# Modulation weights of the second layer in 256 KB pieces, four steps ahead, in a two-layer SSD and S5 block

## The chip, the cores and the metric

The kernel runs on one core of a Trainium2 chip. The metric is the device time of one launch in microseconds (us), as the median of the runs shown. TensorE (PE) does the matrix products, with its weight loads listed apart as PEld; VectorE (DVE), ScalarE (ACT) and GpSimd (POOL) work on tiles in SBUF; SyncE (SP) issues nearly all DMA transfers, in order, and stands still in front of a transfer until its destination is free.

## The reference

Two layers work on 1024 latent tokens and 256 context tokens of width 1024, all in float32. Each layer first turns the conditioning vectors into six modulation vectors, then runs a mixer (SSD and S5 scans) and a gated feed-forward network. What the change touches is the first line, for layer 1:

```python
def ada_params(cvec, w, b):
    return jnp.split(jax.nn.silu(cvec) @ w + b, 6, axis=-1)

sh1, sc1, gt1, sh2, sc2, gt2 = ada_params(c, w_ada[l], b_ada[l])
csh1, csc1, cgt1, csh2, csc2, cgt2 = ada_params(c_ctx[None, :], w_ada[l], b_ada[l])
...
hx = modulate(rmsnorm(x, g_pre_ffn[l]), sh2, sc2)
x = x + gt2[:, None, :] * rmsnorm(conv_ffn(hx, ffn_w_up[l], ffn_conv_w[l], ffn_conv_b[l], ffn_w_down[l], rows), g_post_ffn[l])
```

`w_ada[l]` is 1024 by 6144, which is 24 MB in float32, and it is used for two rows alone (the latent and the context conditioning).

## The kernel before, in words

Large products are split: each operand becomes a high and a low part, and three matmuls (lines 751, 752, 753, called `mm` here) replace one. The feed-forward network of a layer runs over two blocks of tokens. In each block, groups of two or three column tiles of the up-projection (weights `rw`, split into `ws`) alternate with a down-projection of eight output tiles (weights `raw`, split into `wd` or a unit). In layer 0 the blocks have 640 tokens. Block 0's matmuls are 256 and 384 columns wide, block 1's 320.

The modulation of layer 1 is computed in the background of layer 0's feed-forward network: `ada` (line 668) is a generator, and `tick` (line 126), which the network calls once for every second weight tile of the up-projection and once for every output tile of the down-projection, moves it on by one `yield`. Line 1940 queues its first third (column blocks 0 to 3) in block 0, line 1982 the other two thirds (4 to 11) in block 1. Below, these are **stage one** and **stage two**.

A step of `ada` asks for a piece of `w_ada`, and multiplies a piece that was asked for `ahead` steps before. A piece has `n1` blocks of 128 rows by 512 columns. Each block is one matmul with a 128 by 32 stationary tile `cv` that occupies 32 of TensorE's 128 columns (`tile_position=(0, 32 * j)`, with j the block's number modulo 4). In the trace such a float32 matmul stands as two MATMUL records. Before, `n1` is 2 and `ahead` 1: 16 pieces of 512 KB in stage one and 32 in stage two, all into one tile `adaw` that has one buffer. Stage two has `gap` 1, so its steps are two ticks apart.

`self.unit(512)` takes the next of 33 numbered tiles of the activations' pool in SBUF from a list, and `free` puts it back at the list's end. The prologue already loads layer 0's first modulation blocks in that way (`n1` 1, `ahead` 16). Layer 0's other modulation blocks keep the form with `adaw`. A scheduler of the framework then fixes each engine's order of instructions at build time.

Of the kernel before, what the change touches and what calls it, by code (L numbers as in the profile page):

```python
# [98 lines left out]
class Kern:  # L99
# [1425 lines left out]
        return acc  # L1525


    def mods(self, l, cbs, which, par=False, gap=0):
        if par:
            yield from self.params(l, self.sp)  # L1530
        yield from self.ada(l, self.prs[l], cbs, 2, 1, gap)
        for w in which:
            self.modvec(self.prs[l], w)

# [127 lines left out]
    def layer(self, l, H):  # L1662
# [225 lines left out]
        n0, n1 = blks[0][1], blks[1][1]  # L1888
# [48 lines left out]
            fill(i, 100)  # L1937
        self.before = es
        if not last:
            self.bg.append(self.flag("A1", self.mods(1, range(4), ("A1",), True)))  # L1940
        self.fgn = 1 if last else 2
        self.fg = [self.stream(blks[1], md[0], R, pr["G1"], pr["A2"], pr["ada"][:, 24:32], hd[0], pn)]
        H = [[], []]
# [13 lines left out]
        def first_next():  # L1957

            ws.close()
            self.keep, self.tabs = self.open_keep(1), ExitStack()  # L1960
            pt = self.tabs.enter_context(self.pool("tp1", side="right"))
            pa = fs.enter_context(self.pool("s5a1"))

            def small():
                self.tp = yield from self.s5_tables(1, pt, pa)
            self.bg.insert(0, self.flag("s5", small()))
            for k in range(KT):
                H[0].append(self.split_act(load(1)(k), n1, g if k % 2 else nc.vector))
                if k == 5:
                    res.extend(self.residual(blks[1], lambda: self.unit(n1)))  # L1970
                yield
# [6 lines left out]
        if last:  # L1978
            self.fg.append(self.stream_out(blks[0], md[1], R[0], pr["G2"], pn))
            tail, done, fin = self.last_out(blks[1], R[0], pr["G2"], pn)  # L1980
        else:
            self.bg.append(self.mods(1, range(4, 12), ("G1", "A2", "G2"), False, 1))
            self.fg.append(self.stream(blks[0], md[1], R, pr["G2"], self.prs[1]["A1"], self.prs[1]["ada"], hd[1], pn))
            tail, done = first_next(), squares
        acc = self.ffn(l, blks[1], H2[1], LW, new, pr, pg, pw, 8, before, tail, done)
# [133 lines left out]
```

## Time and profile before

| | |
|---|---|
| median of 3 runs | 3443.62 us |
| all runs | 3463.33, 3443.62, 3442.58 us |
| the profiled execution | 3467.04 us |
| its span | 3465.3 us, 48617 instructions |
| mean granted TensorE clock | 0.934 |
| PE busy | 3088.8 us (89%) |
| DVE / ACT / POOL busy | 2060.4 / 1454.7 / 1104.2 us |
| `adaw` transfers | 80 of 512 KB, 48 of them for layer 1 |

The profiled execution is one run with its own time; the 1.7 us between its time and its span lie around the span. A row of the timeline gives the start of an instruction or of a run of equal ones, its length, and in brackets how long the engine had stood idle before it and what ended that. Starts of matmuls are measured; their ends are modelled.

### The profile page before, as it was taken

To read this page: it belongs to the slowest core of one execution; us is meant where nothing else is said; L and a number is where in the kernel's file an instruction comes from. 1 tells how busy PE (TensorE), PEld (TensorE's weight loads), DVE (VectorE), ACT (ScalarE), POOL (GpSimd) and SP (SyncE) were. 2 spreads that over 40 slices of the span, in tenths; PEclk is the share of its full clock that TensorE was granted. 3 is DMA by queue.
4 is the path that set the end of the run, shared out by engine and by line. 5 is a ranking of instruction groups with operands and counts; after the bars stand their busy time and mean duration, and the time that the engine had idled before them with its cause. 6 is when DMAs were issued, how large, how long until landed. Compare 5 with 4: busy or idle time off the path is not lost. (4 is left out here: it accounts for less than half of the span.)

```text
span 3465.3 us, 48617 instructions
## 1 busy us (share of the span) xinstructions
PE 3088.8 (89%) x18067; PEld 2673.7 (77%) x18067; DVE 2060.4 (59%) x3789; ACT 1454.7 (42%) x2610; POOL 1104.2 (32%) x847
## 2 busy tenths in 40 slices
PE   7689796898899999899999879775898999999998
PEld 4578674678879999889999769774576777877876
DVE  4875982456644444653344887993556655566555
ACT  4324522544543434543334443522545544454443
POOL 3651451213312323322222341451233333233230
PEclk8899897889999999999999889886889999999999
DMA  7345378525472222663322426268524533354332
GB/s 234 114 139 178 116 239 212 169 76 159 145 223 77 69 78 75 205 209 115 111 92 75 134 87 202 67 215 193 147 84 145 176 115 93 100 161 121 93 96 72
DMA packets 587281, 468.80 MB, mean 135 GB/s; under 512 B 59076, under 2 KB 506190, under 8 KB 587045
## 3 DMA queue, kind: packets, MB, share of 16 engines
q1 hardware_dynamic: 586565, 465.53, 44.5%
q8 instruction: 142, 2.33, 0.3%
q14 instruction: 94, 0.77, 0.1%
q0 software_dynamic: 480, 0.17, 0.0%
HBM read 355.99 MB, written 109.61 MB: 134 GB/s over the span
## 5 line engine op out<-in xcount | busy, mean ns | idle before, releaser
L860 POOL TENSOR_TENSOR ws<-rw,ws 128x512 fp32r<-128x512 f32 x352 | 483.9, 1377 | 1033.4 <-ACT ws L859 764.0
L752 PE MATMUL mm<-unit,ws 128*128 128x320 f32 (+3 forms) x2112 | 714.8, 338 | 3.4 <-POOL unit L901 3.4
L751 PE MATMUL mm<-unit,ws 128*128 128x320 f32 (+3 forms) x2112 | 716.5, 339 | 0.2 <-ACT unit L900 0.2
L753 PE MATMUL mm<-unit,ws 128*128 128x320 f32 (+3 forms) x2112 | 713.5, 338 | 0.0
L1439 DVE SCALAR_TENSOR_TENSOR fc<-fr,fcols,fc 128x255 f32<-128x255 f32 (+2 forms) x220 | 207.3, 958 | 492.7 <-ACT fc L1432 492.7
L751 PE MATMUL mm<-unit,whi 128*128 128x320 f32 (+3 forms) x1264 | 429.1, 341 | 38.0 <-ACT unit L900 23.4
L753 PE MATMUL mm<-unit,wlo 128*128 128x320 f32 (+3 forms) x1264 | 421.1, 334 | 31.4 <-POOL ub L996 19.0
L751 PEld LDWEIGHTS mm<-unit,ws 128*128 128x128 f32 x2112 | 398.0, 188 | 46.6 <-issue 10.1
L752 PEld LDWEIGHTS mm<-unit,ws 128*128 128x128 f32 x2112 | 398.0, 188 | 36.1 <-POOL unit L901 4.6
L753 PEld LDWEIGHTS mm<-unit,ws 128*128 128x128 f32 x2112 | 397.9, 188 | 34.7 <-issue 3.4
L752 PE MATMUL mm<-unit,whi 128*128 128x320 f32 (+3 forms) x1264 | 421.8, 334 | 2.6 <-POOL unit L901 1.6
L742 POOL TENSOR_TENSOR wlo<-raw,whi 128x1024 fp32r<-128x1024 f32 (+1 forms) x86 | 230.6, 2682 | 361.9 <-ACT whi L741 328.2
L751 PEld LDWEIGHTS mm<-unit,whi 128*128 128x128 f32 x1264 | 253.0, 201 | 74.7 <-ACT unit L900 25.4
L859 ACT CAST ws<-rw 128x512 fp32r<-128x512 f32 x352 | 218.4, 621 | 206.0 <-PE mm L753 116.8
L753 PEld LDWEIGHTS mm<-unit,wlo 128*128 128x128 f32 x1264 | 253.6, 201 | 47.3 <-POOL ub L996 19.2
L1519 DVE TENSOR_TENSOR acc<-mm,acc 128x256 f32<-128x256 f32 (+2 forms) x336 | 185.0, 554 | 171.2 <-PE mm L753 170.3
L752 PEld LDWEIGHTS mm<-unit,whi 128*128 128x128 f32 x1264 | 254.1, 201 | 15.3 <-issue 6.0
L751 PE MATMUL mm<-g,wd 128*128 128x320 f32 (+3 forms) x708 | 243.7, 345 | 10.8 <-ACT wd L859 6.8
L753 PE MATMUL mm<-g,wd 128*128 128x320 f32 (+3 forms) x708 | 241.5, 343 | 6.5 <-DVE wd L860 6.3
L752 PE MATMUL mm<-g,wd 128*128 128x320 f32 (+3 forms) x708 | 242.0, 342 | 0.0
L895 ACT COPY fr<-mm 128x320 f32<-128x320 f32 (+3 forms) x264 | 125.2, 476 | 195.1 <-PE mm L753 194.8
L1441 DVE SCALAR_TENSOR_TENSOR fc<-fr,fcols,fc 128x255 f32<-128x255 f32 (+2 forms) x220 | 176.0, 815 | 3.5
(390 smaller groups left out, 5761.5 us busy)
## 6 DMA issues: line engine op xcount, KB each, us to landing
rw<-in_ffn_w_up_dram SPq DMA_DIRECT2D x352, 256.0 KB
adaw<-in_w_ada_dram SPq DMA_DIRECT2D x80, 512.0 KB
raw<-in_ffn_w_down_dram SPq DMA_DIRECT2D x96, 384.0 KB
raw<-in_w_in_dram SPq DMA_DIRECT2D x40, 512.0 KB
raw<-in_w_out_dram SPq DMA_DIRECT2D x32, 512.0 KB
unit<-in_w_ada_dram SPq DMA_DIRECT2D x32, 256.0 KB
wt<-ws SPq DMA_DIRECT2D x32, 256.0 KB
ct<-w SPq DMA_DIRECT2D x64, 128.0 KB
```

Of the source, the lines that this page charges most:

```text
L742: (eng or nc.vector).tensor_tensor(lo[:, :m], raw[:, :m], hi[:, :m].bitcast(F32), op=OP.subtract)
L751: mm(ps, whi[:, k], ahi[:, sl], start=first and k == 0, stop=False)
L752: mm(ps, whi[:, k], alo[:, sl], start=False, stop=False)
L753: i = mm(ps, wlo[:, k], ahi[:, sl], start=False, stop=last and k == len(a) - 1)
L859: self.nc.scalar.copy(hi, x)
L860: eng.tensor_tensor(lo, x, hi.bitcast(F32), op=OP.subtract)
L895: self.nc.scalar.copy(t[:, o:o + c], x)
L1439: v.scalar_tensor_tensor(cr[:, :, 1:], rr[:, :, :w - 1], f[0][:, ft:ft + 1], cr[:, :, 1:], op0=OP.mult, op1=OP.add)
L1441: v.scalar_tensor_tensor(cr[:, :, :w - 1], rr[:, :, 1:], f[2][:, ft:ft + 1], cr[:, :, :w - 1], op0=OP.mult, op1=OP.add)
L1519: v.tensor_tensor(acc[m][:, o:o + c], ps, acc[m][:, o:o + c], op=OP.add)
```

## The change: four arguments of one generator

`mods` gets two parameters that it hands to `ada`, and the two calls for layer 1 set them to pieces of one block (256 KB) in units, four steps ahead, with one tick for each step in stage two as well. The call for layer 0 keeps the defaults.

```diff
-    def mods(self, l, cbs, which, par=False, gap=0):
+    def mods(self, l, cbs, which, par=False, gap=0, n1=2, ahead=1):
         if par:
             yield from self.params(l, self.sp)
-        yield from self.ada(l, self.prs[l], cbs, 2, 1, gap)
+        yield from self.ada(l, self.prs[l], cbs, n1, ahead, gap)
...
-            self.bg.append(self.flag("A1", self.mods(1, range(4), ("A1",), True)))
+            self.bg.append(self.flag("A1", self.mods(1, range(4), ("A1",), True, 0, 1, 4)))
...
-            self.bg.append(self.mods(1, range(4, 12), ("G1", "A2", "G2"), False, 1))
+            self.bg.append(self.mods(1, range(4, 12), ("G1", "A2", "G2"), False, 0, 1, 4))
```

The order of instructions differs from layer 0's feed-forward network's first group to the end of stage two, and nowhere else. On PE, stage two, in a down-projection of block 1, the kernel before has (`adaw` is the 512 KB tile, `g` and `wd` or `unit` the operands of the down-projection):

```order
L753 MATMUL mm<-g,wd 128x320
L55 MATMUL ps<-adaw,cv 32x512 x2
L751 MATMUL mm<-g,wd 128x320
L752 MATMUL mm<-g,wd 128x320
L753 MATMUL mm<-g,wd 128x320
```

The next such pair follows 36 `mm` rows later. The changed kernel has there, on PE:

```order
L753 MATMUL mm<-g,unit 128x320
L55 MATMUL ps<-unit,cv 32x512
L751 MATMUL mm<-g,wd 128x320
L752 MATMUL mm<-g,wd 128x320
L753 MATMUL mm<-g,wd 128x320
```

The next one follows 18 `mm` rows later: the two members of a pair are pulled apart. Counted over all of PE's order, the 96 modulation matmuls of layer 1 stand in 48 places before, two in each. Now stage one has 25 places (one with six, two with two, the rest with one) and stage two 59 (five with two, the rest with one).

On PE, stage one, two pieces of the difference. The first is in the first down-projection, which has four modulation pairs before and none now:

```order
 L752 MATMUL mm<-g,unit 128x384
 L753 MATMUL mm<-g,unit 128x384
-L55 MATMUL ps<-adaw,cv 32x512 x2
 L751 MATMUL mm<-g,wd 128x256
 L752 MATMUL mm<-g,wd 128x256
```

The second is in the up-projection behind it, which now begins the stage with the place of six:

```order
-L752 MATMUL mm<-unit,ws 128x256
-L753 MATMUL mm<-unit,ws 128x256
-L751 MATMUL mm<-unit,ws 128x256
+L55 MATMUL ps<-unit,cv 32x512 x6
 L752 MATMUL mm<-unit,ws 128x256
 L753 MATMUL mm<-unit,ws 128x256
```

The first modulation matmul moved from the end of the first up-projection to the second up-projection; the `mm` rows with a minus stand elsewhere in the change.

On SP, stage one, around the first down-projection (`raw`: its weights):

```order
-L55 DMA adaw<-in_w_ada_dram 128x2x512
-L1477 DMA raw<-in_ffn_w_down_dram 128x2x256
+L1477 DMA raw<-in_ffn_w_down_dram 128x2x256
+L55 DMA unit<-in_w_ada_dram 128x512 x2
 L1477 DMA raw<-in_ffn_w_down_dram 128x3x256
```

A request for a piece no longer stands ahead of the next down-projection weights here; two requests for units follow them.

## Rows read from the trace of the kernel before

**Rows 1.** The page: busy time, then PE's busy tenths and granted clock in 40 slices.
```profile
PE 3088.8 (89%) x18067; PEld 2673.7 (77%) x18067; DVE 2060.4 (59%) x3789; ACT 1454.7 (42%) x2610; POOL 1104.2 (32%) x847
...
PE   7689796898899999899999879775898999999998
...
PEclk8899897889999999999999889886889999999999
```

**Rows 2.** Busy time by stretch (us): length, engines' busy time, PE's clock, DMA share.
```profile
core 0: us, PE busy (x) PEld busy (x) DVE busy (x) ACT busy (x) POOL busy (x), PEclk, DMA share, GB/s
940.00:1045.00 105.00, 92.36 (x531) 72.77 (x530) 50.23 (x83) 46.41 (x85) 23.45 (x18) 0.95 0.68 215
1437.00:1490.00 53.00, 46.97 (x273) 39.07 (x272) 31.85 (x44) 25.21 (x52) 11.56 (x9) 0.94 0.69 218
1490.00:1755.00 265.00, 264.64 (x1706) 237.58 (x1705) 117.04 (x177) 102.48 (x185) 68.42 (x52) 1.00 0.45 139
```

**Rows 3.** Waits of PE, 935 to 1045 us: total us, times, longest.
```profile
PE ps L55 <- DMA adaw<-in_w_ada_dram: 8.9, 8, 4.2
PE mm L751 <- ACT fr L895: 1.4, 2, 0.7
PE mm L751 <- ACT wd L859: 0.9, 1, 0.9
```

**Rows 4.** Waits of PE, 1437 to 1755 us.
```profile
PE ps L55 <- DMA adaw<-in_w_ada_dram: 5.4, 3, 3.4
PE mm L751 <- ACT wd L859: 0.8, 1, 0.8
```

**Rows 5.** Timeline of SP, 946 to 957 us: issues of transfers.
```profile
948.07 0.38 SPq L55 DMA_DIRECT2D adaw<-in_w_ada_dram  x1
948.79 0.38 SPq L874 DMA_DIRECT2D rw<-in_ffn_w_up_dram  x1
955.53 0.37 SPq L55 DMA_DIRECT2D adaw<-in_w_ada_dram  x1
```

**Rows 6.** Timeline of PE, 953 to 956 us.
```profile
953.57 1.92 PE L55 MATMUL ps<-adaw,cv 128*32 128x512 f32 x4 [4.16 <-DMA adaw<-in_w_ada_dram]
```

**Rows 7.** Busy time by stretch: the four stretches of slow clock behind waits.
```profile
953.40:961.00 7.60, 7.43 (x28) 5.73 (x28) 2.14 (x4) 3.18 (x7) 0.00 (x0) 0.58 0.59 182
996.00:1001.00 5.00, 5.00 (x23) 4.27 (x20) 3.56 (x6) 3.77 (x6) 1.28 (x1) 0.66 0.65 193
1472.50:1476.00 3.50, 3.40 (x10) 1.74 (x11) 1.74 (x3) 0.81 (x3) 0.00 (x0) 0.50 0.22 24
1476.00:1480.00 4.00, 4.00 (x20) 3.84 (x19) 0.43 (x1) 1.66 (x5) 0.00 (x0) 0.67 0.92 306
```

**Rows 8.** Timeline of PE, 1544 to 1546 us: a pair in stage two.
```profile
1544.13 0.31 PE L752 MATMUL mm<-g,wd 128*128 128x320 f32 x1
1544.28 0.31 PE L753 MATMUL mm<-g,wd 128*128 128x320 f32 x1
1544.52 1.05 PE L55 MATMUL ps<-adaw,cv 128*32 128x512 f32 x4
1545.50 0.42 PE L751 MATMUL mm<-g,wd 128*128 128x320 f32 x1
1545.76 0.31 PE L752 MATMUL mm<-g,wd 128*128 128x320 f32 x1
1545.91 0.31 PE L753 MATMUL mm<-g,wd 128*128 128x320 f32 x1
```

**Rows 9.** Timeline of PE, 442 to 444 us: one modulation matmul alone, in layer 0.
```profile
442.21 1.05 PE L55 MATMUL ps<-adaw,cv 128*32 128x512 f32 x2
443.18 0.42 PE L751 MATMUL mm<-unit,whi 128*128 128x320 f32 x1
443.44 0.31 PE L752 MATMUL mm<-unit,whi 128*128 128x320 f32 x1
443.58 0.31 PE L753 MATMUL mm<-unit,wlo 128*128 128x320 f32 x1
```

**Rows 10.** Timeline of PE, 36 to 40 us: four modulation matmuls in a row, in the prologue.
```profile
36.19 1.07 PE L55 MATMUL ps<-unit,cv 128*32 128x512 f32 x8
```

**Rows 11.** DMA, 0 to 60 us: GB/s in 40 slices, and the transfers of `w_ada`.
```profile
GB/s 0 187 182 290 284 306 370 382 382 256 339 372 326 375 390 400 299 317 358 381 410 391 378 377 382 142 116 325 228 291 281 356 376 264 57 209 405 403 398 394
...
unit<-in_w_ada_dram SPq DMA_DIRECT2D x32, 256.0 KB
```

## What I expect, and why

> **What bounds the kernel now.** I read the page first. TensorE is busy for 89% of the span, and in the slices of layer 0's feed-forward network nearly all the time, at full clock [rows 1]. The stretches come next, since only that network changes. From 1490 to 1755 us, most of stage two, PE is busy for 264.64 of 265 us at clock 1.00, DVE for 117 and ACT for 102 [rows 2]. There the bound is PE itself: what is added to its queue lengthens the kernel one for one, and no wait is left to remove. The other two stretches are different: 940 to 1045 us (stage one) has 12.6 us in which PE is not busy, 1437 to 1490 us (the start of stage two) has 6.0 us, and both have a lower clock [rows 2]. Third, the waits: in these stretches PE waits longest for `adaw`, 8.9 us in 8 waits and 5.4 us in 3 [rows 3, 4].
>
> The mechanism of such a wait can be followed in one place. SP asks for a piece at 948.07 us. PE has nothing else to do at 949.4 us, and the matmul starts at 953.57 us, after 4.16 us of idling [rows 5, 6]. The next request goes out at 955.53 us, as PE finishes the matmuls that read the only buffer [rows 5, 6]. One buffer and one step of lead, with a tick as short as one output tile of the down-projection, are too little. Behind such waits, the long ones of 4.16 and 3.4 us and some of the shorter ones, PE runs below full clock: 0.58 for 7.6 us, 0.66 for 5.0 us, 0.50 for 3.5 us, 0.67 for 4.0 us [rows 7]. The two levels are 1.2 and 2.4 GHz, and 0.50 is the lower one.
>
> **The change, part by part.**
>
> *The waits go.* Four steps of lead replace one (stage one) or one of two ticks (stage two), and a new transfer no longer waits for the last matmul. In the down-projection, where ticks are shortest, one tick is 18 `mm` of 0.15 us, 2.7 us, so four are over 10 us; the transfer above took 5.5 us from its request [rows 5, 6]. I take all 8.9 + 5.4 = 14.3 us as gained. The bounds are 0, if something else is late in the same place, and 17.4 us, if the waits for `wd` and `fr` beside them go too (1.4 + 0.9 + 0.8 us more) because SP is no longer held up [rows 3, 4].
>
> *The slow clock goes.* Lost time is length times missing share: 7.6 x 0.42 + 5.0 x 0.34 + 3.5 x 0.50 + 4.0 x 0.33 = 3.2 + 1.7 + 1.75 + 1.3 = 8.0 us [rows 7]. I take all of it, since the waits named precede it; the bounds are 0 and 8.0.
>
> *The pairs come apart.* This is the large term. In a stream of `mm` with 320 columns the starts are 0.15 us apart. Around a pair they are 1544.28, 1545.50, 1545.76 and 1545.91 us: 1.22 us across the pair instead of 0.15, then 0.26 instead of 0.15 [rows 8]. A pair displaces 1.07 + 0.11 = 1.18 us. Its two matmuls cost what one costs: one alone in layer 0 has its start at 442.21, the next `mm` at 443.18 (0.97 us later; behind the pair it is 0.98), and the one after 0.26 us later [rows 9]. Four in a row take 1.07 us [rows 10]. So what PE pays for is places in the queue, with up to four different 32-column strips in each, not matmuls. Nothing else can run in the other strips, as the `mm` use all 128 columns. The order has 48 places before. After, it has 25 + 59 = 84, and the place with six counts as two (strips 0 and 1 occur twice), which makes 85. The addition is 37 x 1.18 = 43.7 us. Its lower bound, without the slower start of the second `mm`, is 37 x 1.07 = 39.6 us. All of it falls into stretches in which PE is the bound.
>
> *The transfers get smaller and there are more of them.* 96 instead of 48 requests cost SP 0.37 us each [rows 5], 18 us more spread over 400 us; SP does not bind, as it mostly stands in front of weight tiles. I cost it at nothing; its cover is the prefetch of `rw` and `raw`. If that were gone, the 18 us would be the price. Bytes stay the same. As to speed, the prologue's 32 pieces of 256 KB run along at 370 to 410 GB/s in many slices, several in flight [rows 11], above the 215 GB/s that stage one has [rows 2].
>
> The Trainium skill, "DMA: Bandwidth & Descriptors" (sections "Anatomy of one DMA" and "Bandwidth"), speaks against the change here: about 2.0 us fixed for each transfer, and batches of 1 MiB or more. By that page, as an estimate, 96 times 2.6 us instead of 48 times 3.2 us is 96 us more if transfers followed one another. The rate in rows 11 says that they overlap, and the trace decides.
>
> *Units.* Five are in use at once, and they come from the end of a list from which layer 0's network holds 16 for its activations and 2 for `wd`. About 15 circulate, so a transfer's destination was last read some 15 steps before. Cost nothing; cover: the length of that list.
>
> *Later end.* Stage one ends about a quarter of a block later on PE. Its result is read in block 1. Cost nothing.
>
> **Sum.** +43.7 - 14.3 - 8.0 = +21.4 us. Against the profiled execution's 3467.0 us this gives 3488.4; that execution lies 23.4 us above the median of the runs, 3443.6, and near the slowest of them. Carried over to the median: 3465 us, 0.6% more. The ends from the bounds: 39.6 - 17.4 - 8.0 = +14 us and +43.7 us with no gain at all, so 3458 and 3487 us.
>
> **Rivals.**
>
> *A. The places cost, but the waits do not pay back (slower).* In the down-projection of both stages PE needs a `wd` tile from ACT, and waits for it just beside the `adaw` waits [rows 3, 4]. If the removed 14.3 us only let PE arrive earlier at weights that are no sooner there, or if those waits are shorter in an execution without the profiler, the 43.7 us stand alone: 3443.6 + 43.7 = 3487 us, +1.3%. It decides from the point at which less than 9.3 us of the 22.3 come back, for then the loss passes 34.4 us (1%). For it: two of the three runs are over 20 us faster than the profiled one, so something in that one was slower. Against: the waits end exactly with `adaw` landing, and the waits for `wd` are an eighth as long. Chance 0.22.
>
> *B. A lone matmul costs half of a pair.* Then the addition is nothing and only the gain stands: 3443.6 - 22.3 = 3421 us, -0.6%. For it: two matmuls are the same work however placed. Against: rows 8 and 9 have 0.98 and 0.97 us. Chance 0.07.
>
> *C. Transfers become the bound.* By the skill's fixed cost, named above. As a mechanism here: each place would wait for its piece, as at 953.57 us. With a wait of 1 us at each of the 85 places, 3465 + 85 = 3550 us. Against: rows 11. Chance 0.02.
>
> *D. The change does not give four steps of lead,* because SP is held up by weight requests ahead of it, or a unit is not yet free. Then the waits come back in stage one at 85 instead of 48 places; the time is A's or a little more, 3495 us. Against: the order on SP puts the requests of the down-projection ahead of, not behind, most `rw`. Chance 0.04.
>
> The forecast itself has 0.65.
>
> **Numbers.** 1% is 34.4 us, about what a measurement of this kernel can tell from no change, with runs 0.6% apart. Slower by over 1% (above 3478 us): most of A (0.18), C and D (0.06), and the forecast's own upper end (0.04), 0.28. Faster by over 1% (below 3409 us): needs B and more, 0.02. Within 1%: 0.70. The range that leaves out no more than 2 in 10 takes in the forecast with its bounds and A with a few us above it, and B is left out: 3445 to 3492 us.
>
> **What would show it.** After the change, PE's waits on `w_ada` transfers in these two stretches should be gone, and the clock there 1.00. The modulation matmuls of layer 1 should stand in 84 places, each with 1.2 us between the `mm` before and the one after; the whole of layer 0's network should be 20 us longer although PE idles less. What would make it wrong: lone matmuls with 0.6 us between neighbours (B), waits for `unit<-in_w_ada_dram` (C, D), or new waits for `wd` of 10 us and more (A).

## The result, and the profile after the change

The changed kernel took 3478.2 us in the median of 7 runs (3472.76 to 3499.43), the kernel before 3456.51 us in the median of 7 runs beside it (3442.58 to 3466.5). The ratio is 1.0086, with a 95% interval from 1.0062 to 1.0109: the change costs 21 to 38 us. The forecast was 0.6%.

The page of the profiled execution, which took 3472.76 us:

```profile
span 3471.0 us, 48663 instructions
...
PE 3110.2 (90%) x18067; PEld 2664.0 (77%) x18067; DVE 2067.9 (60%) x3789; ACT 1454.3 (42%) x2610; POOL 1088.3 (31%) x847
...
PEclk9899897999999999999999989896889999999999
```

Against [rows 1], PE does the same 18067 matmuls and is busy for 21 us longer. The two spans cannot be subtracted: the first 820 us have the same code in both, and were 18.5 us shorter in this execution than in the profiled one of before. So I look for the same matmul in both traces, counted along line 753, and compare the stretches between. From the up-projection just ahead of stage one's first down-projection to behind stage one it was 208.5 us before (932.7 to 1141.2) and is 212.3 now (914.2 to 1126.5): +3.8. From just ahead of stage two's first pair to behind stage two it was 320.9 us (1437.5 to 1758.4) and is 344.2 (1422.6 to 1766.8): +23.3. The forecast had -2.0 and +23.4.

The same waits as in [rows 3, 4], of PE, total us, times, longest. First stage one with the down-projection ahead of it, 920 to 1110 us, in the changed kernel:

```profile
PE mm L751 <- ACT wd L859: 2.8, 1, 2.8
PE mm L751 <- ACT fr L895: 2.5, 1, 2.5
PE mm L753 <- POOL wd L860: 0.5, 1, 0.5
PE mm L753 <- DVE wd L860: 0.4, 1, 0.4
```

Then 1437 to 1755 us:

```profile
PE ps L55 <- DMA unit<-in_w_ada_dram: 1.1, 1, 1.1
PE mm L753 <- DVE wd L860: 0.6, 1, 0.6
```

The 14.3 us of waits for `adaw` have become one wait of 1.1 us. But the waits for `wd` (a split tile of the down-projection's weights) and for `fr` (ACT's copy of an up-projection result, which frees an `mm` buffer), 0.9 and 1.4 us before, are now 2.8 and 2.5; they end at 942.33 and 927.45 us, in the first down-projection. The stretches show what the clock did around them (columns as in [rows 2]; a value between 0.50, the lower level, and 1.00 is the mean of a stretch that holds both):

```profile
926.00:932.00 6.00, 4.55 (x21) 4.55 (x22) 4.15 (x8) 5.49 (x13) 1.54 (x2) 0.72 0.69 199
942.00:949.00 7.00, 6.67 (x27) 6.57 (x28) 2.64 (x6) 3.41 (x9) 0.73 (x1) 0.55 0.95 321
960.00:1105.00 145.00, 145.00 (x852) 118.95 (x851) 64.24 (x106) 54.56 (x93) 35.29 (x27) 1.00 0.40 129
1420.00:1470.00 50.00, 48.34 (x277) 38.72 (x277) 33.87 (x45) 25.24 (x53) 13.02 (x10) 1.00 0.74 233
1470.00:1770.00 300.00, 299.67 (x1753) 247.86 (x1752) 120.93 (x177) 104.26 (x188) 65.77 (x53) 1.00 0.39 125
```

From 960 to 1105 us and from 1470 us on PE has next to no gap, and the clock is full there and from 1420 us on; of the slow stretches in [rows 7] nothing is left there. In the first down-projection two new ones stand, 0.72 for 6 us and 0.55 for 7 us: by length times missing share 6 x 0.28 + 7 x 0.45 = 4.8 us, as much as stage one lost before (4.9).

Last, PE's timeline in stage two, 1600 to 1605.6 us: one place of two and one of one (start, length).

```profile
1600.09 0.31 PE L753 MATMUL mm<-unit,ws 128*128 128x320 f32 x1
1600.32 1.05 PE L55 MATMUL ps<-unit,cv 128*32 128x512 f32 x4
1601.31 0.41 PE L751 MATMUL mm<-g,wd 128*128 128x320 f32 x1
1601.56 0.31 PE L752 MATMUL mm<-g,wd 128*128 128x320 f32 x1
...
1603.90 0.31 PE L753 MATMUL mm<-g,wd 128*128 128x320 f32 x1
1604.14 1.04 PE L55 MATMUL ps<-unit,cv 128*32 128x512 f32 x2
1605.12 0.42 PE L751 MATMUL mm<-g,unit 128*128 128x320 f32 x1
1605.37 0.31 PE L752 MATMUL mm<-g,unit 128*128 128x320 f32 x1
```

From the `mm` before to the one behind it is 1.22 us for two and 1.22 us for one, where neighbouring `mm` are 0.15 apart, and then 0.25 instead of 0.15. One alone displaces 1.07 + 0.10 = 1.17 us, as the pair does.

### The profile page after: what moved, and what is told of

The parts are those of the page before. It is cut to its first block, busy times and chain, and to the rows that moved or that the text cites. A ratio compares the mean times of both kernels' runs of the same rounds, so it can differ in the third digit from the quotient of the medians.

```text
span 3471.0 us, 48663 instructions
## 1 busy us (share of the span) xinstructions
PE 3110.2 (90%) x18067; PEld 2664.0 (77%) x18067; DVE 2067.9 (60%) x3789; ACT 1454.3 (42%) x2610; POOL 1088.3 (31%) x847
## 4 chain that ended last, share of the span: by engine, by line
PE 43%; DVE 12%; DMA 3%; issue 3%; ACT 2%; POOL 1%; SPq 1%; DVEq 0%; POOLq 0%; ACTq 0%
PE mm L751 13%; PE mm L753 12%; PE mm L752 12%; PE ps L55 5%; DVE X L550 1%; DVE sc L545 1%; DVE X L517 1%; DVE fc L1439 1%; DMA xs<-md 1%; SPq L55 1%; DVE sc L548 1%; DVE fc L1441 1%; DVE X L549 1%; PE mm L55 0%; DMA hk<-h 0%
## 5 line engine op out<-in xcount | busy, mean ns | idle before, releaser
L1439 DVE SCALAR_TENSOR_TENSOR fc<-fr,fcols,fc 128x255 f32<-128x255 f32 (+2 forms) x220 | 207.4, 958 | 506.9 <-ACT fc L1432 506.9
L742 POOL TENSOR_TENSOR wlo<-raw,whi 128x1024 fp32r<-128x1024 f32 (+1 forms) x86 | 223.6, 2601 | 358.7 <-ACT whi L741 334.2
L751 PEld LDWEIGHTS mm<-g,wd 128*128 128x128 f32 x708 | 135.3, 191 | 56.2 <-ACT wd L859 18.0
```

Of the source, the lines that this page charges most:

```text
L742: (eng or nc.vector).tensor_tensor(lo[:, :m], raw[:, :m], hi[:, :m].bitcast(F32), op=OP.subtract)
L751: mm(ps, whi[:, k], ahi[:, sl], start=first and k == 0, stop=False)
L1439: v.scalar_tensor_tensor(cr[:, :, 1:], rr[:, :, :w - 1], f[0][:, ft:ft + 1], cr[:, :, 1:], op0=OP.mult, op1=OP.add)
```

## The experiments

All were timed beside the kernel before; ratios are to it. Of a changed line the edits show only the part that differs, and `...` stands for lines left out. The new parameter `pk` is the number of pieces whose matmuls are issued together.

### 1. The change with its pairs kept together

The changed kernel, whose pieces, units and four steps of lead stay. Only the matmuls wait until two pieces are there, and are then issued side by side. PE has 47 places instead of 85.

```diff
-    def ada(self, l, pr, blocks, n1, ahead, gap=0):
+    def ada(self, l, pr, blocks, n1, ahead, gap=0, pk=1):
...
-                if n >= ahead:
-                    i, k0 = todo[n - ahead]
-                    raw = raws.pop(n - ahead)
+                for q in range(n - ahead - pk + 1, n - ahead + 1) if n >= ahead and (n - ahead) % pk == pk - 1 else ():
+                    i, k0 = todo[q]
+                    raw = raws.pop(q)
...
-self.mods(1, range(4), ("A1",), True, 0, 1, 4)
+self.mods(1, range(4), ("A1",), True, 0, 1, 4, 2)
...
-self.mods(1, range(4, 12), ("G1", "A2", "G2"), False, 0, 1, 4)
+self.mods(1, range(4, 12), ("G1", "A2", "G2"), False, 0, 1, 4, 2)
```

> Pieces of 256 KB into units, four steps ahead, as in the change, but the two matmuls of two pieces are issued together again: 47 places on PE (one of six counts as two) instead of 85. My theory (a place costs 1.18 us whatever stands in it, and the waits for adaw and the slow clock behind them were worth 22.3 us): 38 x 1.18 = 45 us less than the change, and 1.2 + 17 to 22 us less than the kernel before, ratio to before 0.993 to 0.995. Rival A (the waits removed are not gained, something else is late): the same as before, ratio 1.000. Rival (the many small transfers cost the time): slower than before by 20 us and more, ratio 1.006 to 1.009 as the change.

Measured: ratio 0.9957 (0.9932 to 0.9981), faster than before by some 15 us (7 to 23). This splits the change in two. Smaller pieces in units with more lead bring 15 us; the places that it adds cost the rest, 1.0086 - 0.9957 = 1.3% (1.0 to 1.6 by the two intervals), 45 us, against 38 x 1.18 = 44.8 us by the trace. Whatever the 48 more requests cost is already taken off these 15 us. No run parts smaller pieces from units and from more lead, so which of them brings the gain stays open.

Between the same matmuls as above, stage one is 10.0 us shorter than before and stage two 5.9, where the forecast's terms, with one place less, give 15.0 and 8.5. The waits of PE, 860 to 1110 us, show what is missing in stage one: the two waits are there too, where no lone matmul is.

```profile
PE mm L751 <- ACT wd L859: 2.7, 1, 2.7
PE mm L751 <- ACT fr L895: 2.6, 1, 2.6
```

### 2. Four together

The same with `pk` at 4, 24 places.

```diff
-False, 0, 1, 4, 2)
+False, 0, 1, 4, 4)
```

> As the pair kernel, but four matmuls of four pieces, one for each 32-column strip, issued together: 24 places on PE. My theory: 24 places fewer than before are 28 us, with the gain of 17 to 22 us from waits 45 to 50 us less than before, ratio 0.985 to 0.987; no wait for a w_ada transfer. Rival (only two run beside each other, or the strips do not matter): as the pair kernel, ratio 0.993 to 0.995. Rival (a batch of four pieces is waited for): between the two, with waits for unit<-in_w_ada_dram in the profile.

Measured: ratio 0.9907 (0.9882 to 0.9932), some 32 us faster than before. PE's timeline in it, 1568 to 1570 us:

```profile
1568.20 0.31 PE L753 MATMUL mm<-g,wd 128*128 128x320 f32 x1
1568.44 1.07 PE L55 MATMUL ps<-unit,cv 128*32 128x512 f32 x8
1569.44 0.41 PE L751 MATMUL mm<-g,unit 128*128 128x320 f32 x1
1569.69 0.31 PE L752 MATMUL mm<-g,unit 128*128 128x320 f32 x1
```

Four cost 1.24 us from `mm` to `mm`, where one costs 1.22. So 96 matmuls in 24 places are paid as 24. By the ratio the gain is less than the 45 to 50 us expected; between the same matmuls the two stages of this one execution are 18.7 and 23.1 us shorter, 41.8 in all. Stage one's two waits and their slow clock are there again (2.6 and 2.4 us, mean clock 0.90 from 926 to 960 us). A third wait stands at the start of stage two, at 1440 us here, and in every later run with fours or eights (waits of PE, 1400 to 1770 us):

```profile
PE mm L753 <- DVE wd L860: 2.8, 1, 2.8
```

### 3. Pairs in the same strip

The kernel before, with its 48 places and 512 KB tiles. Only the strip is chosen otherwise for layer 1, so that the two matmuls of a pair write the same 32 columns. Places, bytes and instructions are the same.

```diff
-j = k % 4
+j = k // 2 if l else k % 4
...
-start=i == 0 and k < 4, stop=i == nb - 1 and k >= 4
+start=i == 0 and (k % 2 == 0 if l else k < 4), stop=i == nb - 1 and (k % 2 == 1 if l else k >= 4)
```

> The kernel before, with layer 1's pairs of modulation matmuls put into one strip of 32 columns (tile_position by k // 2 instead of k % 4); transfers, waits and places as before. My theory (a pair is as cheap as one because its two matmuls stand in different strips): the second matmul of a pair starts only when the first has streamed, 0.85 to 0.9 us later, in 48 places: 41 to 43 us slower than before, ratio 1.012. Rival (the cost of a place is a fixed price of going from the full array to a strip and back, and the matmuls in it cost little): ratio 1.000.

Measured: ratio 1.0104 (1.0082 to 1.0127), 36 us slower (28 to 44). PE's timeline in it, 1712 to 1715 us:

```profile
1712.48 0.31 PE L753 MATMUL mm<-g,wd 128*128 128x320 f32 x1
1712.72 1.90 PE L55 MATMUL ps<-adaw,cv 128*32 128x512 f32 x4
1714.55 0.41 PE L751 MATMUL mm<-g,wd 128*128 128x320 f32 x1
1714.80 0.31 PE L752 MATMUL mm<-g,wd 128*128 128x320 f32 x1
```

A pair in one strip takes 2.07 us from `mm` to `mm`, 0.85 more than a pair in two. So it is the different strips that let two cost as one, not that they stand next to each other. 48 x 0.85 = 41 us; the interval has it.

### 4. and 5. Each stage alone

In experiment 4 only the second call is changed, in experiment 5 only the first.

```diff
-self.mods(1, range(4), ("A1",), True, 0, 1, 4)
+self.mods(1, range(4), ("A1",), True)
```

> Only the second call (stage two, 64 matmuls) gets the change's arguments; stage one stays with adaw and 512 KB. My theory: 27 places more are 31.9 us, less 5.4 us of waits and 3.1 us of slow clock: 23 us slower than before, ratio 1.0068, nearly all of what the change costs. Rival (stage one's new order is what costs): ratio 1.000 to 1.003.

Measured: ratio 1.0065 (1.0041 to 1.0090), 22 us.

```diff
-self.mods(1, range(4, 12), ("G1", "A2", "G2"), False, 0, 1, 4)
+self.mods(1, range(4, 12), ("G1", "A2", "G2"), False, 1)
```

> Only the first call (stage one, 32 matmuls) gets the change's arguments; stage two stays with adaw and 512 KB. By the terms of the prediction: 10 places more are 11.8 us, less 8.9 us of waits and 4.9 us of slow clock, 2 us faster, ratio 0.9995. My theory now, from the profile of the change (5.4 us of new waits for fr and wd in the first down-projection, with slow clock behind them): 4 to 6 us slower, ratio 1.0012 to 1.0018, which with stage two alone makes up the change's 1.0086. Rival (the two stages influence each other): faster than before by 5 us and more, or slower by 10 us and more.

Measured: ratio 1.0018 (0.9999 to 1.0038), 6 us, with 0 just inside. The two add up to 1.0083, where the whole has 1.0086. So there is no sign that one stage acts on the other, though the three intervals together leave room for some 13 us. The forecast's terms were +23.4 for stage two, which holds, and -2.0 for stage one, where +6 (0 to 13) was measured; between the same matmuls stage one of experiment 5's execution is 1.4 us longer than before. The waits of PE in experiment 5, 920 to 1110 us:

```profile
PE mm L751 <- ACT fr L895: 2.8, 1, 2.8
PE mm L751 <- ACT wd L859: 2.6, 1, 2.6
```

### 6. Stage one's pieces begun later

Is it the requests for units that hold up the weights of the first down-projection? Here four stand together, and stage one's modulation begins 12 ticks later, behind that down-projection.

```diff
-    def mods(self, l, cbs, which, par=False, gap=0, n1=2, ahead=1, pk=1):
+    def mods(self, l, cbs, which, par=False, gap=0, n1=2, ahead=1, pk=1, late=0):
...
+        for _ in range(late):
+            yield
         yield from self.ada(l, self.prs[l], cbs, n1, ahead, gap, pk)
...
-True, 0, 1, 4, 4)
+True, 0, 1, 4, 4, 12)
```

> The kernel with fours in units, stage one begun 12 ticks later, so that no request for w_ada stands on SP before or in the first down-projection. It asks why PE waits there 2.4 to 2.8 us for wd and 2.6 us for fr, which the kernel before has at 0.9 and 1.4 us. Theory T (the requests for units compete with the down-projection's weights, on the queue or in transfer): the wait for wd falls under 1 us, and the kernel is 3 to 6 us faster than the fours without the delay, ratio 0.989. Theory P (PE comes earlier to work that is no earlier, since no modulation matmul stands in that phase any more): both waits stay within 0.5 us of 2.4 and 2.6 us, ratio 0.9907 as the fours.

Measured: ratio 0.9898 (0.9870 to 0.9926), not to be told from experiment 2. Its waits of PE, 920 to 1110 us, and SP's timeline, 930 to 955 us:

```profile
PE mm L751 <- ACT fr L895: 2.9, 2, 2.8
PE mm L751 <- ACT wd L859: 2.8, 1, 2.8
```

```profile
946.24 0.32 SPq L55 DMA_DIRECT2D xd<-xs  x1
946.62 0.42 SPq L55 DMA_DIRECT2D xs<-md  x1
948.05 0.32 SPq L55 DMA_DIRECT2D xk<-xd  x1
948.41 0.95 SPq L1477 DMA_DIRECT2D raw<-in_ffn_w_down_dram  x2
```

Both waits stand there, though no request for `w_ada` goes out on SP before 958.68 us, when that down-projection ends. My theory that the units' requests were in the way falls. What stands ahead of the request for `raw` is block 0's other background work, the generator `stream`: the store of `xd`, the load of `xs`, the load of `xk`.

### 7. Eight together

As experiment 2 with `pk` at 8: 12 places, each with two matmuls in every strip.

```diff
-False, 0, 1, 4, 4)
+False, 0, 1, 4, 8)
```

> Eight modulation matmuls of eight pieces together, two to each strip: 12 places. From the place of six in the change (1.91 + 0.1 us) and the same-strip pair (1.93 + 0.1 us), a second round adds 0.85 us to a place of 1.18 us: 12 x 2.03 = 24.4 us instead of 24 x 1.18 = 28.3 us, 4 us less than the fours, ratio 0.9895. Rival (each round of four costs a whole place): ratio 0.9907 as the fours. Rival (eight pieces in hand are waited for): above the fours, with waits for unit<-in_w_ada_dram.

Measured: ratio 0.9884 (0.9862 to 0.9907), 40 us faster. PE's timeline, 1575 to 1578 us:

```profile
1575.10 0.31 PE L753 MATMUL mm<-g,wd 128*128 128x320 f32 x1
1575.34 1.92 PE L55 MATMUL ps<-unit,cv 128*32 128x512 f32 x16
1577.19 0.42 PE L751 MATMUL mm<-g,unit 128*128 128x320 f32 x1
```

The second round costs 2.09 - 1.24 = 0.85 us, as in experiment 3. A place costs 1.17 us with one round and 0.85 more for each further one, so about 0.3 us of it is paid for the interruption alone. Against experiment 2 that would be 12 x 0.3 = 4 us, within the intervals of both. Between the same matmuls the two stages took 189.8 + 297.8 us with fours and 188.5 + 298.9 with eights: no gain of eights over fours is shown.

### 8. The other background work moved behind

As experiment 7, and `stream` begins 28 yields (14 ticks) later, so that its stores and loads no longer stand on SP among the first down-projection's weights.

```diff
-self.fg = [self.stream(blks[1], md[0], R, ...)]
+self.fg = [itertools.chain(iter(range(28)), self.stream(blks[1], md[0], R, ...))]
```

> The kernel with eights in units, and the other background work of block 0 (stream, which loads, scales and stores the tiles xs and xk) begun 14 ticks later, so that none of its transfers stands on SP ahead of the first down-projection's weights, and none of its work on DVE and ACT ahead of the gate. Theory P1 (PE waits 2.7 us for wd and 2.6 us for fr in that phase because the weights' requests stand behind stream's stores on SP, and ACT's copies behind DVE's work for stream): both waits fall under 1 us, the slow clock behind them goes, 6 to 9 us faster than the eights, ratio 0.986. Theory P2 (they wait for other work, the gate's own chain on DVE and ACT): the wait for fr stays at 2 us and more, the wait for wd falls, ratio 0.9875. Rival (stream's work is only moved and costs later what it saves): waits of 5 us and more elsewhere before 1110 us, ratio 0.9884.

Measured: ratio 0.9872 (0.9852 to 0.9893), 44 us faster than before, but not separable from experiment 7. SP's request for the late weights, PE's waits, 915 to 1110 us, and two stretches:

```profile
935.89 0.38 SPq L1477 DMA_DIRECT2D raw<-in_ffn_w_down_dram  x1
```

```profile
PE mm L751 <- DVE acc L1519: 3.4, 1, 3.4
PE ps L55 <- DVE rs L251: 1.1, 1, 1.1
PE mm L751 <- ACT fr L895: 0.4, 1, 0.4
```

```profile
915.00:945.00 30.00, 30.00 (x205) 29.96 (x204) 14.68 (x24) 17.90 (x40) 9.44 (x8) 1.00 0.51 156
1003.00:1012.00 9.00, 8.32 (x47) 5.79 (x48) 7.28 (x14) 2.42 (x5) 1.02 (x1) 0.81 0.67 197
```

Here it is shown that `stream` causes stage one's waits: with it out of the way the wait for ACT's `wd` is gone, the one for `fr` is 0.4 us, and PE is busy throughout the down-projection at clock 1.00. Between the same matmuls that stretch is 9.2 us shorter than in experiment 7. By which of its parts `stream` does it, its requests on SP or its work on DVE and ACT, this run does not say, as it moves them all. The gain doesn't last: where the delayed work now stands, PE waits 3.4 us for `acc` from DVE, the clock goes to 0.81, and by 1030 us 9.4 us have been given back. That it is late work of `stream` on DVE that delays `acc` fits the place, but no run isolates it.

## Why the prediction held, and the term that was off

**The bound.** PE bounds stage two, as it did: 264.64 us busy of 265 before [rows 2], 299.67 of 300 now, at clock 1.00 in both. What was added to its queue lengthened that stage by as much: 27 x 1.18 - 5.4 - 3.1 = 23.4 us by the forecast's terms, +23.3 between the same matmuls.

**The pairs come apart** (+43.7 us). This holds, from three sides. In the trace one alone and a pair both take 1.22 us from `mm` to `mm`, as [rows 8, 9] had it. The difference between the change and experiment 1 is 45 us. Stage two alone costs 22 us for a sum of 23.4. The reason that I gave, up to four strips beside each other, holds in both directions: four in four strips cost what one does (experiment 2), two in one strip cost 0.85 us more (experiment 3). The Trainium skill, "TensorEngine Tiling (Array Packing)", section "Key Properties", says that tiles of the array take weights and matmuls in parallel, and that a change of the tiling mode drains the engine. The first agrees with the rows: up to four strips cost 1.24 us as one costs 1.22. The second would fit the some 0.3 us of each place that don't depend on the number of rounds, but no run isolates that these are a drain.

**Rival B** (a lone matmul costs half of a pair) is out by the same rows. **Rival C** (transfers become the bound) is out by the waits: 1.1 us in all for `w_ada` instead of 85. The estimate by the Trainium skill's "DMA: Bandwidth & Descriptors", section "Anatomy of one DMA", which makes 96 us of the smaller transfers, assumes that they follow one another, and that section's figures are for transfers which GpSimd issues, where SP issues these. Here, with several in flight, it doesn't hold; experiment 1 has as many of them and is faster than before. **Rival D** (no four steps of lead) is out: no wait for a piece in stage one.

**The waits and the slow clock go** (-14.3 and -8.0 us). This is the term that was mis-sized: 22.3 us forecast, some 14 by experiment 1 (5 to 22 by its interval, so the ratio alone hardly excludes 22.3; its 15 us hold one place less) and 14.7 between the same matmuls. In the change's stage two nearly all of it came: the waits for pieces went from 5.4 to 1.1 us, and its clock is 1.00. In stage one the 8.9 us of waits and the two slow stretches went, and in the first down-projection came 2.8 us for `wd`, 2.5 us for `fr` and two stretches of slow clock worth 4.8 us. That is rival A's mechanism, in part: counted from the end of the up-projection, PE came to the `wd` tile 9.0 us earlier than before, and the tile was ready only 7.1 us earlier, so the wait grew from 0.9 to 2.8 us. The prediction took the waits for `wd` beside `adaw` as something that could only go, with SP less held up. Why the tile is not there sooner still can be followed in the changed kernel, on SP, ACT and DVE:

```profile
934.78 0.33 SPq L55 DMA_DIRECT2D xd<-xs  x1
935.15 0.43 SPq L55 DMA_DIRECT2D xs<-md  x1
936.58 0.32 SPq L55 DMA_DIRECT2D xk<-xd  x1
936.95 0.44 SPq L1477 DMA_DIRECT2D raw<-in_ffn_w_down_dram  x1
```

```profile
941.88 0.40 ACT L859 CAST wd<-raw 128x256 fp32r<-128x256 f32 x1 [1.85 <-DMA raw<-in_ffn_w_down_dram]
```

```profile
933.40 1.35 DVE L1556 SCALAR_TENSOR_TENSOR xs<-xs,G,xk 128x640 f32<-128x640 f32 x1
934.67 0.41 DVE L860 TENSOR_TENSOR wd<-raw,wd 128x256 fp32r<-128x256 f32 x1
```

SP issues in order. The load of `xk` reads what the store of `xd` writes, and goes out 1.80 us after it; the request for `raw` is next in line, lands just before 941.88 us, and ACT has stood idle for 1.85 us by then. The queue is not all of it. `raw` has two buffers, and DVE reads the one that this request fills until 935.08 us, right behind 1.35 us of `stream`'s work (line 1556). The request goes out 1.87 us after that, and ACT can start 4.93 us later. In experiment 8, in which nothing of `stream` stands ahead, the same read ends at 935.87 us, the request goes out at 935.89, ACT starts 3.14 us later, and the wait is gone. So `stream` delays these weights by its work on DVE as well as by its place in SP's queue, and perhaps in the time that the transfer takes (4.93 against 3.14 us to ACT's start). No run parts these. Before the change PE stood in front of `adaw` in this down-projection for up to 4.16 us at a time [rows 6], and weights came meanwhile. What [rows 3] show could not tell how late they would be without that: a wait shows only what ended last.

**Stage one's sum.** By the rows: +11.8 for ten places, -11.2 + 6.2 for all waits named (before by [rows 3], after as above), and -4.9 + 4.8 for the clock, +6.7 us. Before, PE had two more waits in that stretch that [rows 3] leave out, 1.1 us for `rs` and 0.3 for `acc`, and after there are none such, which makes it +5.3. Measured: +3.8 between the same matmuls, 6 us (0 to 13) by experiment 5. Some 1.5 us between the sum and the stretch stay unassigned.

**The numbers.** 3465 us was carried over from a median of three runs, 3443.62. Beside the change the kernel before had 3456.51 in seven. Of the 13 us between forecast and result nearly all is that base; the difference itself is 21.7 us between the medians and 30 (21 to 38) by the ratio, against 21.4; between the same matmuls, from ahead of stage one to behind stage two, it is 852.6 - 825.7 = 26.9 us. So the size came out near, at the lower end of the interval: the mis-sized term left it some 8 us short by the ratio. Over that same stretch experiment 1 is 16.4 us shorter than before, experiment 2 40.8, experiment 7 42.3 and experiment 8 43.0.

**A version that beats both.** The change's good half, smaller pieces in units with more lead, with four or eight matmuls to a place: experiments 2, 7 and 8, 0.99 to 0.987 of the time before. Layer 0's modulation, with lone matmuls as in [rows 9], was not tried in this form.

## What to carry to other kernels

Where small matmuls that use only a strip of the array are sprinkled into a full queue of wide ones, count the places where the queue is interrupted, not the matmuls, and collect as many as there are strips: splitting a transfer need not split the issue of its matmuls. Before a wait is booked as gained, look at what the engine needs next and follow that one's request back to the queue it stands in and to the buffer it fills: the wait that you remove may have been its cover. A change with two halves of opposite sign is best judged by a run that has only one of them.

## What the runs showed of the hardware

Float32 matmuls of 32 columns by 512, between full matmuls that are 0.15 us apart: one, two or four in different strips all take 1.22 to 1.24 us from neighbour to neighbour, two in the same strip 2.07, eight in four strips 2.09. PE's clock fell around short waits: with the one of 2.5 us and behind the one of 2.8 us the mean granted clock was 0.72 over 6 us and 0.55 over 7 us (1.00 and 0.50 are the two levels), so the slow clock cost nearly as much (4.8 us) as the waits themselves (5.3 us).
